# Where the tiles lie in a partition: pools reordered and padded to multiples of 2048 bytes

## The chip, the core and the metric

The kernel runs on one core of a Trainium2 chip. The metric is the device time of one execution in microseconds. Before the change it is 2291.4 us, the median of three runs (2290.7 to 2291.65).

## What is computed

A decoder trunk of two layers on one sequence of 256 positions and 2048 channels, in float32. Each layer normalizes x, projects it with one wide matrix to the queries, keys and values of four kinds of attention (latent, dilated window, forgetting, stick-breaking; four heads of 128 each), joins them through an output projection, and adds a gated FFN of width 5632. Cut to what matters:

```
for l in range(DEPTH):                       # 2 layers
    h = rms_norm(x, attn_norm[l])
    proj = h @ w_in[l]                       # 2048 -> q, k, v of four mixers
    groups = rms_norm(stack(mla, dilated, forgetting, stick_breaking), group_norm[l])
    x = x + groups @ w_out[l]                # 2048 -> 2048
    h = rms_norm(x, ffn_norm[l])
    x = x + (silu(h @ w_gate[l]) * (h @ w_up[l])) @ w_down[l]   # 2048 -> 5632 -> 2048
return rms_norm(x, final_norm)
```

## The kernel before, in words

All 256 positions are held at once, channels on the partitions. The float32 products are made of parts: each operand is split into a high part, rounded to the type float32r, and the low rest, and three of the four partial products are summed in PSUM. So an activation tile holds high and low beside each other (XS for the normalized input of a layer's half, h for everything else that is multiplied: latents, group outputs, FFN activations), and a weight tile comes as a pair wh and wl.

`load` (line 197) fetches the weights in order from one long array: 1 MB at a time into a `raw` tile of 2048 elements for each partition, by SP's queue. ACT then copies it, rounded, to wh (L213), and DVE subtracts to get wl (L214), in two halves of 1024 elements. raw has three buffers, wh and wl four each, so loads run ahead of the matmuls.

All big products go through `Acc.mm` (its matmul is L230), and come in three shapes:

- `wide` (line 241): one weight block of 128x128 is stationary; the moving operand is 512 columns (high and low of an activation) for wh, then 256 columns (the high part) for wl. Used for queries and keys, gate, up and down, and most of the output projection.
- `narrow` (line 234): the same with three matmuls of 256 columns: high and low with wh, high with wl. Used for the latents and for the last quarter of the output and the last chunk of the down projection (`last_out`, line 649, which accumulates in att tiles).
- `proj_v` (line 282): the values. Here the activation is stationary and 512 columns of wh or wl are the moving operand.

FFN: `gate_up` (line 667) makes the h tiles of a chunk of the hidden width from XS (six chunks, of 8 times 128 channels, the last of 4), and the down product of a chunk, with h moving, comes after the next chunk's gate and up.

The pools are opened in lines 170 to 175, and a pool's tiles lie one behind the other in each partition, pools in the order of opening, each tile rounded up to 32 bytes. In the program as built, the first tile X0 starts at byte 16512. That gives these starts before the change:

| tiles | pool | bytes each | first start | past a multiple of 2048 | past a multiple of 64 |
|---|---|---|---|---|---|
| X (8) | cp | 2048 | 16512 | 128 | 0 |
| XS (8) | cp | 4096 | 32896 | 128 | 0 |
| sm, cst, exact | cp | 520, 10264, 1040 | 65664, 66208, 76480 | 128, 672, 704 | 0, 32, 0 |
| raw (3) | rawp | 8192 | 77536 | 1760 | 32 |
| wh, wl (4 each) | wp | 4096 | 102112 | 1760 | 32 |
| h (7) | hp | 4096 | 134880 | 1760 | 32 |
| q4 (4), og | qp | 4096 | 163552 | 1760 | 32 |
| the rest | tp | | 184032 | 1760 | 32 |

All tiles of a pool from rawp to qp have a size that is a multiple of 2048, so all of them lie at the same place as the first.

Of the kernel before, what the change touches and what calls it, by code (L numbers as in the profile page):

```python
# [8 lines left out]
F32 = mybir.dt.float32  # L9
F32R = mybir.dt.float32r  # L10
# [13 lines left out]
LNEXP = "natural_log_exp_and_others"  # L24
SC_A = 192 ** -0.5
SC = 128 ** -0.5
RAW_B, W_B, H_B, Q_B4, OG_B, T2, SG = 3, 4, 7, 4, 1, 3, 3
CH = [8, 8, 8, 8, 8, 4]

# [8 lines left out]
SM_N = SM_FIN + 16  # L38
# [4 lines left out]
C_N = 2566  # L43
# [122 lines left out]
def trunk(ctx: ExitStack, tc: tile.TileContext, x_d, w_d, sm_d, c_d, out_d):  # L166
    nc = tc.nc
    V, A, P = nc.vector, nc.scalar, nc.tensor

    cp = ctx.enter_context(tc.tile_pool(name="cp", bufs=1))  # L170
    rawp = ctx.enter_context(tc.tile_pool(name="rawp", bufs=RAW_B))
    wp = ctx.enter_context(tc.tile_pool(name="wp", bufs=W_B))
    hp = ctx.enter_context(tc.tile_pool(name="hp", bufs=H_B))
    qp = ctx.enter_context(tc.tile_pool(name="qp", bufs=Q_B4))
    tp = ctx.enter_context(tc.tile_pool(name="tp", bufs=2))
    accp = ctx.enter_context(tc.tile_pool(name="accp", bufs=2, space=bass.MemoryType.PSUM))
    attp = ctx.enter_context(tc.tile_pool(name="attp", bufs=4, space=bass.MemoryType.PSUM))

    A.preload_act_table_set(LNEXP)

    X = [cp.tile([128, 2, S], F32, name=f"X{i}") for i in range(8)]
    XS = [cp.tile([128, 2, 2, S], F32R, name=f"XS{i}") for i in range(8)]
    sm = cp.tile([128, SM_N], F32, name="sm")
    cst = cp.tile([128, C_N], F32, name="cst")

    ones = cst[:, C_ONE:C_ONE + 128]
    ident = cst[:, C_ID:C_ID + 128]
    tri = cst[:, C_TRI:C_TRI + 128]

    exact = cp.tile([128, 260], F32R, name="exact")  # L190
    ones_r = exact[:, :128]
    tri_r = exact[:, 132:]

# [67 lines left out]
    def proj_pair(src, nk, per):  # L261
        acc = Acc()
        k = 0
        while k < nk:
            n = min(per, nk - k)
            blk = load(n * 256)
            for kk in range(n):
                for t in range(2):
                    acc.wide(t, blk(kk * 256 + t * 128, 128), src(k), k == nk - 1)
                k += 1  # L270
        return acc

    def proj_quad(src, nk, unit=None, acc=None):
        acc = acc or Acc()
        for k0 in range(0, nk, 4):
            blk = (unit or load)()
            for kk in range(4):
                for t in range(4):
                    acc.narrow(t, blk(kk * 512 + t * 128, 128), src(k0 + kk), k0 + kk == nk - 1)
        return acc.t  # L280
# [17 lines left out]
    def sumsq(srcs):  # L298
        tot = None
        for s in srcs:  # L300
            sq = tp.tile([128, 2, S], F32, name="sq", tag="sg", bufs=SG)
            A.activation(sq, s, AF.Square)
            if tot is None:
                tot = sq
            else:
                V.tensor_add(tot, tot, sq)
        V.tensor_add(tot[:, 0, :], tot[:, 0, :], tot[:, 1, :])
        return tot

    def rsq(tot, n, name, more=None):  # L310
        ps = attp.tile([128, 512], F32, name="att")
        if more is None:
            hl = tp.tile([128, 2, S], F32R, name="ss_hl", tag="hl", bufs=1)
            A.activation(hl[:, 0, :], tot[:, 0, :], AF.Copy)
            V.tensor_sub(hl[:, 1, :], tot[:, 0, :], hl[:, 0, :].bitcast(F32))
            parts, one = [hl[:, 0, :], hl[:, 1, :]], ones_r
        else:
            parts, one = [tot[:, 0, :], *more], ones
        for i, p in enumerate(parts):
            P.matmul(ps[:, :S], one, p, start=i == 0, stop=i == len(parts) - 1)  # L320
        a, ln = tot[:, 1, :], tot[:, 0, :]
        V.tensor_scalar(a, ps[:, :S], 1.0 / n, EPS, op0=OP.mult, op1=OP.add)
        A.activation(ln, a, AF.Ln)
        r0 = tp.tile([128, S], F32, name="rq_r", bufs=1)
        A.activation(r0, ln, AF.Exp, scale=-0.5)
        V.tensor_mul(ln, r0, r0)
        V.scalar_tensor_tensor(a, ln, -0.5, a, op0=OP.mult, op1=OP.mult)
        r = tp.tile([128, S], F32, name=name, bufs=1)
        V.scalar_tensor_tensor(r, a, 1.5, r0, op0=OP.add, op1=OP.mult)
        return r  # L330

    def rcol(r, name):
        ps = attp.tile([128, 512], F32, name="att")
        for t in range(2):
            P.matmul(ps[:, t:t + 1], r[:, t * 128:t * 128 + 128], cst[:, C_SEL + 4:C_SEL + 5],
                     start=t == 0, stop=True, skip_group_check=True)
        c = tp.tile([128, 2], F32, name=name, bufs=1)
        V.tensor_copy(c, ps[:, :2])
        return c

    def split_x(i, g0):
        for t in range(2):
            g = sm[:, g0 + 2 * i + t:g0 + 2 * i + t + 1]
            A.activation(XS[i][:, t, 0, :], X[i][:, t, :], AF.Copy, scale=g)  # L344
            V.scalar_tensor_tensor(XS[i][:, t, 1, :], X[i][:, t, :], g,
                                   XS[i][:, t, 0, :].bitcast(F32),
# [18 lines left out]
    def softmax_heads(qk_mm, vt, scale, mask, o):  # L365
        st = []
        for h in range(4):
            s = tp.tile([128, 384], F32, name="sm_s", bufs=4)
            m = mask(h, s)
            ps = attp.tile([128, 512], F32, name="att")  # L370
            qk_mm(h, ps)
            V.scalar_tensor_tensor(s, ps[:, :384], scale, m, op0=OP.mult, op1=OP.add)
            st.append(s)
        blocks = (slice(0, 128), slice(128, 384))
        for s in st:
            nm = tp.tile([128, 2], F32, name="sm_nm", bufs=4)
            rs = tp.tile([128, 2], F32, name="sm_rs", bufs=4)
            for b, sl in enumerate(blocks):
                V.tensor_reduce(nm[:, b:b + 1], s[:, sl], AX.X, OP.max, negate=True)
            for b, sl in enumerate(blocks):  # L380
                A.activation(s[:, sl], s[:, sl], AF.Exp, bias=nm[:, b:b + 1],
                             accum_out=rs[:, b:b + 1])
            ri = tp.tile([128, 2], F32, name="sm_ri", bufs=4)
            V.reciprocal(ri, rs)
            for b, sl in enumerate(blocks):
                V.tensor_scalar(s[:, sl], s[:, sl], ri[:, b:b + 1], None, op0=OP.mult)
        pst = []
        for s in st:
            pt = attp.tile([128, 512], F32, name="att")
            for j in range(3):  # L390
                P.transpose(pt[:, j * 128:j * 128 + 128], s[:, j * 128:j * 128 + 128], ident)  # L391
            p = tp.tile([128, 384], F32, name="sm_p", bufs=4)
            A.activation(p, pt[:, :384], AF.Copy)
            pst.append(p)
        for h in range(4):
            pv(pst[h], vt, h, o[:, h, :])
# [9 lines left out]
    def qk_plain(qt, kt):  # L406
        def f(h, ps):
            P.matmul(ps[:, :128], qt[:, h, :128], kt[:, h, :128], start=True, stop=True,  # L408
                     skip_group_check=True)
            P.matmul(ps[:, 128:384], qt[:, h, 128:], kt[:, h, :], start=False, stop=True,  # L410
                     skip_group_check=True)
        return f
# [15 lines left out]
    def stick_heads(qt, kt, vt, o):  # L428
        zs, es = [], []
        for h in range(4):  # L430
# [5 lines left out]
            z = tp.tile([128, 384], F32, name="sm_s", bufs=4)  # L436
            V.scalar_tensor_tensor(z, ps[:, :384], SC, cst[:, C_MD:C_MD + 384],
                                   op0=OP.mult, op1=OP.add)
# [21 lines left out]
    def group(og, l, g):  # L460
        tot = sumsq([og[:, 0:2, :], og[:, 2:4, :]])
        r = rsq(tot, GW, "r_g")
        gs = [hp.tile([128, 2, 2, S], F32R, name="h") for _ in range(2)]
        for t in range(4):
            gain = sm[:, l * SM_L + SM_GRP + 4 * g + t:l * SM_L + SM_GRP + 4 * g + t + 1]
            V.scalar_tensor_tensor(og[:, t, :], og[:, t, :], gain, r, op0=OP.mult, op1=OP.mult)
        for t in range(0, 4, 2):
            split(gs[t // 2], og[:, t:t + 2, :])
        return lambda k: gs[k // 2][:, k % 2]

    for l in range(DEPTH):
        sb = l * SM_L
        acc = Acc()
        if l == 0:
            nc.scalar.dma_start(sm, sm_d)

            def first_unit(c=[0]):
# [4 lines left out]
                def x_in(j):  # L482
                    i = i0 + (j - 1 if first else j)
                    if i0 <= i < i0 + 2:
                        nc.sync.dma_start(X[i], x_d[:, 2 * i:2 * i + 2, :])

# [10 lines left out]
        else:  # L497
            proj_quad(xk, KT, None, acc)
        rx = rsq(sumsq(X), D, "r_x")
        rxc = rcol(rx, "rxc")  # L500
# [87 lines left out]
        og = qp.tile([128, 4, S], F32, name="og", bufs=OG_B)  # L588
        softmax_heads(qk_plain(qb, kb), vb, SC, lambda h, s: cst[:, C_MB:C_MB + 384], og)
        grp[1] = group(og, l, 1)  # L590
# [44 lines left out]

        softmax_heads(qk_plain(qc, kc), vc, SC, mask_c, og)
        grp[2] = group(og, l, 2)
# [8 lines left out]
        for p in range(8):  # L646
            proj_pair(lambda k: grp[k // 4](k % 4), 12, 6).add_to(X[p])

# [87 lines left out]
```

## Time and profile before

| | |
|---|---|
| median of three runs | 2291.4 us |
| span of the profiled execution, first to last instruction | 2289.3 us |
| TensorE matmul busy | 2270.7 us (99%) |
| TensorE weight load busy | 2011.0 us (88%) |
| VectorE (DVE) busy | 1538.9 us (67%) |
| ScalarE (ACT) busy | 1107.7 us (48%) |
| bytes moved by DMA | 419.79 MB, mean 183 GB/s |

The profile gives the profiled execution's own time as its span; the median is that of other runs, 2.1 us above it. Matmuls are pipelined: a row's duration overlaps with the next matmul's, and its end is modelled. How fast TensorE really goes is therefore read from the starts of successive matmuls. A tile name such as `acc<-h,wh` names the output, then the moving operand, then the stationary one.

### The profile page before, as it was taken

What the parts mean: (1) busy time and instruction counts of PE and PEld (TensorE: products, weight loads), DVE (VectorE), ACT (ScalarE), POOL (GpSimd) and SP (SyncE); (2) the same over time, 40 slices, a digit from 0 to 9 for tenths busy, and PEclk for the clock granted to TensorE, in tenths of its full rate; (3) what the DMA queues carried; (4) which work ended last, traced back from release to release, by engine and by line L of the source; (5) the groups of instructions that cost most, each with busy time, mean ns of one, the idle gap of its engine ahead of it and who ended that gap; (6) DMA issues with size and microseconds to landing.
All of it is one profiled execution on the core that took longest, in us unless ns stands there. A gap on an engine that the chain in (4) does not pass through costs nothing.

```text
span 2289.3 us, 32935 instructions
## 1 busy us (share of the span) xinstructions
PE 2270.7 (99%) x13462; PEld 2011.0 (88%) x13462; DVE 1538.9 (67%) x1951; ACT 1107.7 (48%) x1425; POOL 0.2 (0%) x4
## 2 busy tenths in 40 slices
PE   8999999999999999999999999999999999999997
PEld 8888889888888888888998988898888888888887
DVE  7876767766656666666777866686656666666666
ACT  6454555544444444444554545565443444444444
POOL 0000000000000000000000000000000000000000
PEclk9999999999999999999999999999999999999999
DMA  7444445555555555555555444455555555555553
GB/s 282 175 166 166 166 149 197 188 192 195 184 185 189 197 184 185 194 189 187 184 185 191 142 173 157 154 203 187 193 193 184 186 190 194 185 186 195 190 184 111
DMA packets 61638, 419.79 MB, mean 183 GB/s; under 512 B 6832, under 2 KB 7088, under 8 KB 14768
## 3 DMA queue, kind: packets, MB, share of 16 engines
q1 hardware_dynamic: 61344, 417.63, 51.2%
q8 instruction: 106, 1.74, 0.3%
q14 instruction: 44, 0.36, 0.0%
q10 hardware_dynamic: 144, 0.07, 0.0%
HBM read 415.57 MB, written 2.10 MB: 182 GB/s over the span
## 4 chain that ended last, share of the span: by engine, by line
PE 99%; DVE 0%; DMA 0%; ACT 0%; DVEq 0%; issue 0%; SPq 0%; ACTq 0%
PE acc L230 92%; PE att L230 4%; PE att L401 1%; PE att L391 0%; PE att L402 0%; PE att L410 0%; PE att L320 0%; DMA X<-in_x_dram 0%; DVE X L701 0%; PE att L408 0%; PE att L422 0%; PE att L432 0%; PE att L424 0%; PE att L629 0%; PE att L420 0%; PE att L434 0%
## 5 line engine op out<-in xcount | busy, mean ns | idle before, releaser
L214 DVE TENSOR_TENSOR wl<-raw,wh 128x1024 fp32r<-128x1024 f32 (+1 forms) x810 | 964.1, 1193 | 657.3 <-ACT wh L213 655.8
L213 ACT ACTIVATE wh<-raw 128x1024 fp32r<-128x1024 f32 (+1 forms) x810 | 838.2, 1036 | 1084.1 <-PE acc L230 953.6
L230 PE MATMUL acc<-XS,wh 128*128 128x512 f32 (+1 forms) x4160 | 1352.0, 377 | 6.3 <-ACT XS L344 6.3
L230 PE MATMUL acc<-XS,wl 128*128 128x256 f32 x3872 | 1086.8, 281 | 0.0
L230 PEld LDWEIGHTS acc<-XS,wh 128*128 128x128 f32 x4160 | 762.6, 188 | 152.8 <-ACT XS L344 6.3
L230 PEld LDWEIGHTS acc<-XS,wl 128*128 128x128 f32 x3872 | 728.5, 188 | 1.0
L230 PE MATMUL acc<-h,wh 128*128 128x512 f32 (+1 forms) x1824 | 619.0, 389 | 0.0
L230 PE MATMUL acc<-h,wl 128*128 128x256 f32 x1744 | 490.9, 281 | 0.0
L230 PEld LDWEIGHTS acc<-h,wh 128*128 128x128 f32 x1824 | 337.9, 188 | 76.3
L230 PEld LDWEIGHTS acc<-h,wl 128*128 128x128 f32 x1744 | 330.0, 189 | 0.3
L230 PE MATMUL acc<-wh,XS 128*128 128x512 f32 x384 | 122.1, 397 | 0.0
L255 DVE TENSOR_TENSOR X<-X,acc 128x512 f32<-128x512 f32 x96 | 66.0, 687 | 44.1 <-PE acc L230 43.8
L230 PE MATMUL att<-h,wh 128*128 128x256 f32 x512 | 92.3, 283 | 0.0
L230 PEld LDWEIGHTS acc<-wh,XS 128*128 128x128 f32 x384 | 72.1, 188 | 17.7
L230 PEld LDWEIGHTS att<-h,wh 128*128 128x128 f32 x512 | 79.9, 192 | 0.2
L251 DVE TENSOR_TENSOR hilo<-acc,lo 128x512 f32<-128x512 f32 x112 | 76.6, 684 | 0.2
L230 PE MATMUL acc<-wl,XS 128*128 128x512 f32 x192 | 75.3, 392 | 0.0
L230 PE MATMUL att<-h,wl 128*128 128x256 f32 x256 | 72.5, 283 | 0.0
L256 DVE TENSOR_TENSOR X<-X,acc 128x512 f32<-128x512 f32 x96 | 65.9, 686 | 2.7
L249 ACT ACTIVATE lo<-acc 128x512 f32<-128x512 f32 x112 | 64.8, 579 | 0.0
L230 PEld LDWEIGHTS att<-h,wl 128*128 128x128 f32 x256 | 49.2, 192 | 0.0
L230 PEld LDWEIGHTS acc<-wl,XS 128*128 128x128 f32 x192 | 36.1, 188 | 8.3
(147 smaller groups left out, 895.9 us busy)
## 6 DMA issues: line engine op xcount, KB each, us to landing
raw<-in_w_dram SPq DMA_DIRECT2D x364, 1024.0 KB, 4.8
raw<-in_w_dram SPq DMA_DIRECT2D x32, 768.0 KB, 4.4
raw<-in_w_dram SPq DMA_DIRECT2D x8, 512.0 KB, 7.8
X<-in_x_dram SPq DMA_DIRECT2D x8, 256.0 KB, 7.1
out_dram<-X SPq DMA_DIRECT2D x8, 256.0 KB, 2.4
cst<-in_const_dram SPq DMA_DIRECT2D x1, 1216.0 KB, 8.9
raw<-in_w_dram SPq DMA_DIRECT2D x4, 256.0 KB, 4.9
cst<-in_const_dram SPq DMA_DIRECT2D x1, 67.0 KB, 7.4
```

What stands on the lines that cost most here:

```text
L213: A.activation(wh[:, i:e], raw[:, o + i:o + e], AF.Copy)
L214: V.tensor_sub(wl[:, i:e], raw[:, o + i:o + e], wh[:, i:e].bitcast(F32))
L230: P.matmul(out, lhsT, rhs, start=bank not in self.started, stop=stop, skip_group_check=True)
L249: A.activation(tmp, self.t[:, :, 1, :], AF.Copy)
L251: V.tensor_add(out, self.t[:, :, 0, :], tmp)
L255: V.tensor_add(x, x, self.t[:, :, 0, :])
L256: V.tensor_add(x, x, self.t[:, :, 1, :])
L401: P.matmul(po[:, :S], vt[0][:, hs], p[:, :S], start=True, stop=False, skip_group_check=True)
```

## The change

Two pools are added. sp, opened first, takes sm and exact, which were in cp, and a tile PAD of 80 float32 that nothing uses; kp, opened between qp and tp, takes cst, which was in cp too. cp keeps X and XS.

```diff
+PAD = 80
+    sp = ctx.enter_context(tc.tile_pool(name="sp", bufs=1))
     cp = ctx.enter_context(tc.tile_pool(name="cp", bufs=1))
     rawp = ctx.enter_context(tc.tile_pool(name="rawp", bufs=RAW_B))
     wp = ctx.enter_context(tc.tile_pool(name="wp", bufs=W_B))
     hp = ctx.enter_context(tc.tile_pool(name="hp", bufs=H_B))
     qp = ctx.enter_context(tc.tile_pool(name="qp", bufs=Q_B4))
+    kp = ctx.enter_context(tc.tile_pool(name="kp", bufs=1))
     tp = ctx.enter_context(tc.tile_pool(name="tp", bufs=2))
...
+    sm = sp.tile([128, SM_N], F32, name="sm")
+    exact = sp.tile([128, 260], F32R, name="exact")
+    sp.tile([128, PAD], F32, name="pad")
     X = [cp.tile([128, 2, S], F32, name=f"X{i}") for i in range(8)]
     XS = [cp.tile([128, 2, 2, S], F32R, name=f"XS{i}") for i in range(8)]
-    sm = cp.tile([128, SM_N], F32, name="sm")
-    cst = cp.tile([128, C_N], F32, name="cst")
+    cst = kp.tile([128, C_N], F32, name="cst")
...
-    exact = cp.tile([128, 260], F32R, name="exact")
```

## Rows read from the trace of the kernel before

**Rows 1.** The page: span, busy us of each engine, share, instructions.

```profile
span 2289.3 us, 32935 instructions
PE 2270.7 (99%) x13462; PEld 2011.0 (88%) x13462; DVE 1538.9 (67%) x1951; ACT 1107.7 (48%) x1425; POOL 0.2 (0%) x4
```

**Rows 2.** The page: the chain that ended last, share by engine, by line.

```profile
PE 99%; DVE 0%; DMA 0%; ACT 0%; DVEq 0%; issue 0%; SPq 0%; ACTq 0%
PE acc L230 92%; PE att L230 4%; PE att L401 1%; PE att L391 0%; PE att L402 0%; PE att L410 0%; PE att L320 0%; DMA X<-in_x_dram 0%; DVE X L701 0%; PE att L408 0%; PE att L422 0%; PE att L432 0%; PE att L424 0%; PE att L629 0%; PE att L420 0%; PE att L434 0%
```

**Rows 3.** Waits of PE: engine and line, what for, total us, times, longest.

```profile
PE acc L230 <- ACT XS L344: 6.3, 1, 6.3
```

**Rows 4.** Groups by form: shapes, count, busy us, mean ns, idle before.

```profile
L230 PE MATMUL acc<-XS,wh 128*128 128x512 f32 x3584 | 1247.5, 392 | 0.0
L230 PE MATMUL acc<-XS,wl 128*128 128x256 f32 x3872 | 1086.8, 281 | 0.0
L214 DVE TENSOR_TENSOR wl<-raw,wh 128x1024 fp32r<-128x1024 f32 x762 | 932.5, 1225 | 650.5 <-ACT wh L213 649.0
...
L230 PEld LDWEIGHTS acc<-XS,wh 128*128 128x128 f32 x4160 | 762.6, 188 | 152.8 <-ACT XS L344 6.3 <-DVE XS L345 0.2
...
L230 PE MATMUL acc<-h,wh 128*128 128x512 f32 x1664 | 589.1, 399 | 0.0
L230 PE MATMUL acc<-h,wl 128*128 128x256 f32 x1744 | 490.9, 281 | 0.0
...
L230 PE MATMUL acc<-wh,XS 128*128 128x512 f32 x384 | 122.1, 397 | 0.0
L230 PE MATMUL acc<-XS,wh 128*128 128x256 f32 x576 | 104.6, 284 | 6.3 <-ACT XS L344 6.3
L230 PE MATMUL att<-h,wh 128*128 128x256 f32 x512 | 92.3, 283 | 0.0
...
L230 PE MATMUL acc<-wl,XS 128*128 128x512 f32 x192 | 75.3, 392 | 0.0
L230 PE MATMUL att<-h,wl 128*128 128x256 f32 x256 | 72.5, 283 | 0.0
L230 PEld LDWEIGHTS acc<-wh,XS 128*128 128x128 f32 x384 | 72.1, 188 | 17.7
...
L230 PE MATMUL acc<-h,wh 128*128 128x256 f32 x160 | 29.9, 286 | 0.0
```

**Rows 5.** PE in order of time, gate and up: start us, us, what.

```profile
701.63 0.39 PE L230 MATMUL acc<-XS,wh 128*128 128x512 f32 x1
...
704.75 0.39 PE L230 MATMUL acc<-XS,wh 128*128 128x512 f32 x1
```

**Rows 6.** PE in order of time, down.

```profile
725.71 0.40 PE L230 MATMUL acc<-h,wh 128*128 128x512 f32 x1
...
728.89 0.40 PE L230 MATMUL acc<-h,wh 128*128 128x512 f32 x1
```

**Rows 7.** The chain in order of time: start us, us, what.

```profile
1119.13 23.04 PE att L230 x192
1142.17 22.53 PE acc L230 x192
```

**Rows 8.** PE in order of time, proj_v of the first mixer (x2: two merged).

```profile
109.66 0.63 PE L230 MATMUL acc<-wh,XS 128*128 128x512 f32 x2
...
112.46 0.63 PE L230 MATMUL acc<-wh,XS 128*128 128x512 f32 x2
```

**Rows 9.** Stretches with XS, h, proj_v: length, then busy by engine, clock, DMA.

```profile
630.00:710.00 80.00, 80.00 (x464) 70.43 (x463) 48.06 (x50) 37.94 (x43) 0.00 (x0) 1.00 0.54 189
718.00:758.00 40.00, 40.00 (x228) 34.73 (x228) 28.20 (x32) 15.48 (x15) 0.00 (x0) 1.00 0.53 185
108.00:127.00 19.00, 19.00 (x83) 15.27 (x82) 11.04 (x13) 7.42 (x7) 0.00 (x0) 1.00 0.56 193
```

**Rows 10.** DMA issues: count, KB each, median us from issue to landing.

```profile
raw<-in_w_dram SPq DMA_DIRECT2D x364, 1024.0 KB, 4.8
```

## The prediction, made before the changed kernel ran

> **What bounds the kernel now.** I read the page's totals first. TensorE is busy for 2270.7 of 2289.3 us, DVE for 67%, ACT for 48%, and the granted clock is 1.00 in the stretches I read [rows 1, 9]. A busy TensorE alone proves little, since the ends of matmuls are modelled, so the chain comes next: it puts 99% of the span on PE and 96% on the one matmul of line 230 [rows 2]. The waits say the same from the other side: PE's one real wait is 6.3 us for the first XS tile at the start [rows 3]. Nothing that feeds PE is ever late. So only two things can move the time: the number of matmuls, which the change leaves alone, and the time from the start of one matmul to the start of the next, which an address might touch.
>
> The durations by form give the first hint that it does [rows 4]. The same 512-column product takes 392 ns when the moving operand is an XS tile and 399 ns when it is an h tile, from the same weight tiles. These durations overlap and their ends are modelled, so I take start-to-start times instead. With XS moving, nine pairs of a 512- and a 256-column matmul take from 701.63 to 704.75: 3.12/9 = 0.3467 us a pair [rows 5]. With h moving, nine pairs take from 725.71 to 728.89: 3.18/9 = 0.3533 [rows 6]. The same split stands in the 256-column products: the chain's stretch of 192 with h takes 23.04 us, 0.1200 each, and that of 192 with XS right behind it 22.53 us, 0.1173 each [rows 7]. The reader is to see a constant toll on h of 6.7 ns a pair and 2.7 ns a narrow matmul, in stretches where PE never waits.
>
> What differs? By the addresses listed ahead, XS starts 128 bytes past a multiple of 2048, while h, wh and wl start 1760 past one, which is 32 bytes past a multiple of 64. Three things could therefore be the cause: the 32 bytes, the fact that h lies at the same place in 2048 as the weights that PE loads beside it, or something that has nothing to do with addresses. A third kind of stretch tells them apart. In proj_v a wh or wl tile is the moving operand and XS the stationary one, so the moving operand has the 32 bytes but lies at another place than its partner. Four rounds of three 512-column matmuls take from 109.66 to 112.46: 2.80/12 = 0.2333 us each [rows 8]. XS at its own rate would need 0.3467 - 0.1173 = 0.2294, h at its own 0.3533 - 0.1200 = 0.2333. proj_v runs at h's rate to the last digit. So I read the toll as one on a moving operand that starts 32 bytes past a multiple of 64. Crossing a 2048 boundary is not it: both halves of an h tile, 1760 (crosses) and 736 (does not), sit in the 0.1200 stretch.
>
> **The change, part by part.** No instruction is added, removed or given a new wait; PAD is never written or read. What moves is addresses. sp holds sm (520 bytes, 544 with rounding), exact (1040, 1056) and pad (320): 1920 in all, so cp starts at 16512 + 1920 = 18432 = 9 x 2048, and X, XS, raw, wh, wl, h, q4 and og all follow at multiples of 2048. cst now stands ahead of tp, which starts 320 bytes later; 320 is a multiple of 64, so tp's tiles keep their 32 bytes and their rates.
>
> 1. Wide products with h moving: 1664 pairs [rows 4] fall from 0.3533 to 0.3467: 1664 x 0.0066 = 11.0 us.
> 2. Narrow products with h moving: 512 + 160 with wh, and for each two of them one with wl (256 + 80): 1008 matmuls, from 0.1200 to 0.1173: 1008 x 0.0027 = 2.7 us.
> 3. proj_v: 384 + 192 matmuls, from 0.2333 to 0.2294: 576 x 0.0039 = 2.2 us. The 48 of the latent values belong here too (0.2 us, within the rounding).
> 4. Products with XS moving go from 128 past 2048 to 0 past it. Both are multiples of 128, so I take 0. Bounds: below nothing by as much as h's toll, 0.0066 on 3584 pairs (23.7 us less) if there were a second step of the same size between 128 and 2048; above nothing by as much, under the first rival.
> 5. The stationary side: wh and wl lose their 32 bytes too. The weight loads take 188 ns whether the tile is wh (32 bytes off) or XS (not off) [rows 4], and proj_v with its aligned weights showed no gain over h without. So I take 0; the bound is again one toll for each pair, (3584 + 1664) x 0.0066 = 34.6 us.
> 6. DVE, ACT and DMA see raw, wh, wl and h at new places. Whatever they gain or lose is hidden by PE: they are at 58 to 71% (DVE), 39 to 47% (ACT) and 0.53 to 0.56 (DMA) in the stretches read [rows 9], and the raw transfer takes 4.8 us against more than 5 us of PE work on one [rows 10]: 16 pairs are 5.55 us. When PE needs 5.55 instead of 5.65 us for such a load, the cover shrinks by 2%. If it went, the next thing late would be DVE's subtraction into wl, whose 1.2 us for a half tile [rows 4] stands against 2.8 us of PE work. Only the 6.28 us before the first matmul are bare to DMA; a transfer 10% faster or slower would move the time by 0.5 us.
> 7. The q4 tiles in attention's float32 products. No aligned row stands beside these, so I take 0 with bounds. All lines but 230 hold 4% of the chain, 92 us [rows 2]; h's toll is 2% of a pair, and on half of these 92 us it would be 1 us either way.
>
> Sum: 11.0 + 2.7 + 2.2 = 15.9 us. The trace's span of 2289.3 becomes 2273.4. The median of the timed runs is 2291.4, 2.1 us above that span; I keep these 2.1 us, since nothing at either end changes: **2275.5 us**, 0.7% less. That one's own range is 2270 to 2280, for which the small terms 6 and 7 and some reading error of the intervals (0.5 ns on the 1664 + 1008 + 576 slow pairs and matmuls, 1.6 us) are taken together.
>
> [...] The trace shows 0.3467 against 0.3533 us for tiles that are all at multiples of 32 bytes [rows 5, 6]. [...]
>
> **The rivals.**
>
> Same place, slower. What slows h could be that it lies at the same place in 2048 as the weights loaded beside it. Then XS, which now has its own place, is brought there too, and would pay h's toll: 3584 x 0.0066 = 23.7 us on the pairs, (576 + 288) x 0.0027 = 2.3 us on its narrow matmuls, with nothing gained elsewhere: 2291.4 + 26 = 2317. It decides from the first gate_up stretch on, where the pair would read 0.3533. For it: h does lie at its weights' place. Against it: proj_v pays the toll although its two operands, 1760 against 128 and steps of 512 from it, never lie nearer than 96 bytes [rows 8]. I give it 8%.
>
> Not the address at all. h's toll could come from what runs beside it: in its stretch DVE is busy for 28.2 of 40 us, with XS for 48.1 of 80 [rows 9]. Then nothing moves: 2291.4. Against it, proj_v has the toll with DVE at 11.0 of 19 us, less than XS has [rows 9]. The case that the allocation comes out otherwise than I reckoned, so that tiles still lie off, ends here too. 11%.
>
> Weights as well. If the stationary side pays a toll of its own that only shows where the moving side is clean, bound 5 comes on top: 2275.5 - 34.6 = 2241. Rows 4 and 8 speak against it. 9%.
>
> Half of it. The toll goes from some of the three kinds alone, say h's pairs keep theirs or only they lose it: 2280 to 2287, 6%.
>
> **How the numbers follow.** The forecast has 66%, and 2275.5 is its time. About 0.2%, 4.6 us, is the least that a measurement of this kernel can tell from no change. Faster by more than that: the forecast, weights as well, and most of the half cases, 0.80. Within it: not the address, 0.11. Slower: same place and what I have not thought of, 0.09. The range for 8 in 10 goes from 2262, which takes in a part of the weights' case, to 2292, which takes in no change; the slower case and the far end of the weights' case stay outside.
>
> **What would show it.** In the changed trace the pairs with h moving should start 0.3467 apart, as those with XS do, the 192 narrow matmuls should take 22.5 us, not 23.04, and proj_v's 0.229 each; XS's pairs should stay at 0.3467, and the weight loads at 188 ns. The forecast is wrong if XS's pairs read 0.3533 (same place), if h's stay there (not the address), if XS's fall (weights), or if the order of matmuls is another one.

## The result: slower, 2309.5 us

The changed kernel takes 2309.54 us (median of five runs, 2308.89 to 2310.01), the kernel before 2291.4: a ratio of 1.008 with a 95% interval of 1.0068 to 1.0093. That is 18.1 us more, where 15.9 less were forecast. The time lies outside the predicted range and on the other side. In both traces every engine executes the same instructions in the same order, PE's long wait is still the 6.3 us at the start, and the granted clock is 0.998; what differs is the addresses.

The page after has the span and the busy time of each engine. Against [rows 1], PE grew by 18.3 us, DVE by nothing.

```profile
span 2307.3 us, 32935 instructions
PE 2289.0 (99%) x13462; PEld 2015.5 (87%) x13462; DVE 1538.9 (67%) x1951; ACT 1106.3 (48%) x1425; POOL 0.2 (0%) x4
```

The groups by form (shapes, count, busy us, mean ns) answer to [rows 4]; L230 is now L234. The 512-column product with XS moving went from 392 to 398 ns, the one with h stayed at 399, and that of proj_v fell from 397 to 389. The weight loads are within 1 ns of where they were.

```profile
L234 PE MATMUL acc<-XS,wh 128*128 128x512 f32 x3584 | 1267.6, 398 | 0.0
...
L234 PEld LDWEIGHTS acc<-XS,wh 128*128 128x128 f32 x4160 | 764.3, 189 | 169.6 <-ACT XS L348 6.3 <-DVE XS L349 0.2
L234 PE MATMUL acc<-h,wh 128*128 128x512 f32 x1664 | 589.3, 399 | 0.0
...
L234 PE MATMUL acc<-wh,XS 128*128 128x512 f32 x384 | 119.3, 389 | 0.0
```

PE in order of time, three stretches of the changed kernel (start us, us, what): gate and up with XS moving, down with h moving, proj_v.

```profile
700.70 0.40 PE L234 MATMUL acc<-XS,wh 128*128 128x512 f32 x1
...
703.88 0.40 PE L234 MATMUL acc<-XS,wh 128*128 128x512 f32 x1
...
730.03 0.40 PE L234 MATMUL acc<-h,wh 128*128 128x512 f32 x1
...
733.21 0.40 PE L234 MATMUL acc<-h,wh 128*128 128x512 f32 x1
```

```profile
109.73 0.62 PE L234 MATMUL acc<-wh,XS 128*128 128x512 f32 x2
...
112.45 0.62 PE L234 MATMUL acc<-wh,XS 128*128 128x512 f32 x2
```

Nine pairs take 3.18 us in both of the first two: 0.3533 a pair, XS now as slow as h, which did not move [rows 5, 6]. Four rounds of proj_v take 2.72 us, 0.2267 a matmul, quicker than the 0.2333 of [rows 8].

The chain of waits of the kernel before, then of the changed one, has the whole FFN but its last product as one unbroken stretch. It shows where the time went.

```profile
422.89 696.25 PE acc L230 x3992
```

```profile
422.80 705.25 PE acc L234 x3992
1128.05 23.04 PE att L234 x192
1151.08 23.04 PE acc L234 x192
```

The stretch holds 1356 pairs with XS and 640 with h. It grew by 9.00 us, and so did its twin in the second layer: 18.0 us, as much as the span. The narrow products with h stayed at 23.04, those with XS rose from 22.53 to 23.04 [rows 7].

One thing does not fit a simple toll. In the same changed kernel, an earlier stretch with XS moving, from the same tiles' places and the same weight buffers' places, runs fast. PE in order of time:

```profile
90.22 0.39 PE L234 MATMUL acc<-XS,wh 128*128 128x512 f32 x1
...
93.34 0.39 PE L234 MATMUL acc<-XS,wh 128*128 128x512 f32 x1
```

Nine pairs in 3.12 us: 0.3467. At the same addresses within 256 bytes, both rates occur.

### The profile page after: what moved, and what is told of

Its sections match the earlier page's. It is cut to its first block, busy times and chain, and to the rows that moved or that the text cites. A ratio compares the mean times of both kernels' runs of the same rounds, so it can differ in the third digit from the quotient of the medians.

```text
span 2307.3 us, 32935 instructions
## 1 busy us (share of the span) xinstructions
PE 2289.0 (99%) x13462; PEld 2015.5 (87%) x13462; DVE 1538.9 (67%) x1951; ACT 1106.3 (48%) x1425; POOL 0.2 (0%) x4
## 4 chain that ended last, share of the span: by engine, by line
PE 99%; DVE 0%; DMA 0%; ACT 0%; DVEq 0%; issue 0%; SPq 0%; ACTq 0%
PE acc L234 92%; PE att L234 4%; PE att L405 1%; PE att L395 0%; PE att L406 0%; PE att L414 0%; PE att L324 0%; DMA X<-in_x_dram 0%; DVE X L705 0%; PE att L412 0%; PE att L426 0%; PE att L436 0%; PE att L428 0%; PE att L633 0%; PE att L424 0%; PE att L438 0%
## 5 line engine op out<-in xcount | busy, mean ns | idle before, releaser
L234 PE MATMUL acc<-XS,wh 128*128 128x512 f32 (+1 forms) x4160 | 1373.6, 383 | 6.3 <-ACT XS L348 6.3
L234 PE MATMUL acc<-XS,wl 128*128 128x256 f32 x3872 | 1090.2, 282 | 0.0
L234 PEld LDWEIGHTS acc<-XS,wh 128*128 128x128 f32 x4160 | 764.3, 189 | 169.6 <-ACT XS L348 6.3
L234 PEld LDWEIGHTS acc<-XS,wl 128*128 128x128 f32 x3872 | 733.0, 189 | 1.1
L234 PE MATMUL acc<-h,wh 128*128 128x512 f32 (+1 forms) x1824 | 619.2, 389 | 0.0
L234 PE MATMUL acc<-h,wl 128*128 128x256 f32 x1744 | 490.7, 281 | 0.0
L234 PEld LDWEIGHTS acc<-h,wh 128*128 128x128 f32 x1824 | 337.9, 188 | 76.7
L234 PEld LDWEIGHTS acc<-h,wl 128*128 128x128 f32 x1744 | 329.7, 189 | 0.3
L234 PE MATMUL acc<-wh,XS 128*128 128x512 f32 x384 | 119.3, 389 | 0.0
L234 PE MATMUL att<-h,wh 128*128 128x256 f32 x512 | 92.3, 283 | 0.0
L234 PEld LDWEIGHTS acc<-wh,XS 128*128 128x128 f32 x384 | 72.1, 188 | 15.2
L234 PEld LDWEIGHTS att<-h,wh 128*128 128x128 f32 x512 | 79.8, 192 | 0.2
L234 PE MATMUL acc<-wl,XS 128*128 128x512 f32 x192 | 74.8, 389 | 0.0
L234 PE MATMUL att<-h,wl 128*128 128x256 f32 x256 | 72.4, 283 | 0.0
L234 PEld LDWEIGHTS att<-h,wl 128*128 128x128 f32 x256 | 49.2, 192 | 0.0
L234 PEld LDWEIGHTS acc<-wl,XS 128*128 128x128 f32 x192 | 36.0, 188 | 7.3
```

The costliest lines, as they stand in the source:

```text
L234: P.matmul(out, lhsT, rhs, start=bank not in self.started, stop=stop, skip_group_check=True)
```

## The experiments

In what follows the distance of a product is the start of its stationary tile minus that of its moving tile, modulo 256. (All blocks of weights, halves of XS and h and so on are steps of multiples of 512, so a product has one distance.) Before, XS had 96, h 0, proj_v 160; in the changed kernel all three have 0. Where a kernel was timed once only, that is marked (one run); the kernel before took 2291.4 (2291.1, 2291.3) us beside them. Repeated runs of one kernel lie within 1.9 us of each other, so larger differences are not chance, and the granted clock was 0.998 in every run.

### All tiles 32 bytes later

```diff
-PAD = 80
+PAD = 88
```

> All tiles from X to og of the changed kernel 32 bytes later, so that XS, wh, wl and h start 32 bytes past a multiple of 2048, all at the same place. Theory P (same place: a moving tile pays 6.7 ns a pair when it starts at the same place, within some block, as the weight tile loaded beside it): nothing changes against the changed kernel, 2309 us, pairs with XS and with h moving 0.3533 us, proj_v 0.227 each. Theory A (own alignment: XS pays because it now starts at a multiple of 2048 itself, or the weights because they start at a multiple of 64): the start is off again, XS pairs return to 0.3467, 2285 to 2291 us.

Measured: 2282.1 us (one run), below both kernels. Both theories missed it. The chain's stretch for the FFN and for the narrow products with XS:

```profile
422.64 691.95 PE acc L234 x3992
...
1137.62 23.04 PE acc L234 x192
```

Narrow products and proj_v (0.227) are exactly as in the changed kernel, as same place said. But the FFN takes 691.95: all 1996 pairs, XS's and h's alike, at 0.3467. So theory P falls in the form in which it was put, and A hardly explains h, which gained as well, or the narrow products, which did not. With the next three runs this led to a third theory, a lock (L in the expectations): at distance 0 two rates hold, and something at the start of a stretch decides which.

### Weights 32 bytes after XS, h 32 after the weights

```diff
+    g0 = ctx.enter_context(tc.tile_pool(name="g0", bufs=1))
+    g0.tile([128, 8], F32, name="gap0")
     rawp = ctx.enter_context(tc.tile_pool(name="rawp", bufs=RAW_B))
...
+    g1 = ctx.enter_context(tc.tile_pool(name="g1", bufs=1))
+    g1.tile([128, 8], F32, name="gap1")
     hp = ctx.enter_context(tc.tile_pool(name="hp", bufs=H_B))
```

> The changed kernel with 32 bytes ahead of raw and 32 more ahead of h: XS at 0, wh and wl at 32, h at 64 past a multiple of 2048. P: XS and h both lie 32 bytes from the weights, both pairs read 0.3467, narrow products 0.1173, proj_v back to 0.2333; 2291.4 - 13.7 = 2278 us. A: XS still starts at a multiple of 2048 and keeps 0.3533; about 2305 to 2310 us.

Measured: 2300.4 us (one run). The chain: FFN, narrow with h, narrow with XS.

```profile
423.57 700.95 PE acc L238 x3992
1124.53 22.40 PE att L238 x192
1146.93 22.72 PE acc L238 x192
```

h at distance 224 is fast (0.3467 a pair, and 22.40/192 = 0.1167 a narrow matmul, better than anything before). XS at 32 is slow, 0.3533, in every stretch of the FFN (one stretch of 21 pairs in a mixer read 0.3469). So being apart is not enough: the two signs of 32 bytes differ. Theory A looked right on XS here, and wrong on h; neither theory had the time.

### Gaps of 64 and 128 bytes

The same edit with 16 and 32 floats in the two gaps.

> 64 bytes ahead of raw and 128 ahead of h: XS at 0, wh and wl at 64, h at 192. P asks how large the block is within which places are compared: if it is 64 bytes, XS and h are both at the same place as the weights and all is as in the changed kernel, 2309 us with pairs at 0.3533; if it is 128, XS is clear (0.3467) and h not (0.3533), 2291 us; if it is 256 or more, both are clear, 2278 us. A: XS keeps 0.3533, 2305 to 2310 us.

Measured: 2303.3 us (one run).

```profile
421.32 703.77 PE acc L238 x3992
1125.09 22.79 PE att L238 x192
1147.87 21.80 PE acc L238 x192
```

XS at distance 64: 0.3533 a pair, yet its narrow products are the quickest of all, 21.80/192 = 0.1135. h at 128: 0.3511 and 0.1187. None of the three cases of theory P came: h's 0.3511 is neither of its rates. But a distance of 128 is not one of 0, so if places are compared within a block, it is larger than 128.

### Gaps of 256 and 512 bytes, XS where it was before

```diff
     cp = ctx.enter_context(tc.tile_pool(name="cp", bufs=1))
+    g0 = ctx.enter_context(tc.tile_pool(name="g0", bufs=1))
+    g0.tile([128, 64], F32, name="gap0")
     rawp = ctx.enter_context(tc.tile_pool(name="rawp", bufs=RAW_B))
...
+    g1 = ctx.enter_context(tc.tile_pool(name="g1", bufs=1))
+    g1.tile([128, 128], F32, name="gap1")
     hp = ctx.enter_context(tc.tile_pool(name="hp", bufs=H_B))
...
-    sp = ctx.enter_context(tc.tile_pool(name="sp", bufs=1))   # was first; now behind qp, without PAD
```

> XS back at 128 as in the kernel before (sm, exact, cst behind og), 256 bytes ahead of raw, 512 ahead of h: wh and wl 256 from XS, h 512 from the weights. P: block of 64, 128 or 256 bytes: both at the same place, 2309 us; block of 512: XS clear, h not, 2291 us; block of 1024 or 2048: both clear, 2278 us. A: XS is where it was before the change, so 0.3467 and 2291 us or less.

Measured: 2309.9 us (one run).

```profile
422.88 705.25 PE acc L237 x3992
...
1151.16 23.04 PE acc L237 x192
```

256 and 512 bytes apart is as good as 0: the FFN stretch has the changed kernel's 705.25 to the last digit, proj_v its 0.227. XS starts at 128 past 2048, as before the change, and is slow all the same, so A falls on XS too. As far as these runs go, the period is 256 bytes.

### sm and exact swapped

Only these two small tiles change place; everything from X to tp stays on the changed kernel's addresses.

```diff
-    sm = sp.tile([128, SM_N], F32, name="sm")
     exact = sp.tile([128, 260], F32R, name="exact")
+    sm = sp.tile([128, SM_N], F32, name="sm")
```

> The changed kernel with sm and exact swapped: exact starts 32 bytes earlier within 256 than in the changed kernel, all tiles from X to tp stay where the change put them, on multiples of 2048. Theory L (lock): the rate hangs on the distance of the stationary from the moving tile, modulo 256; at distance 0 two rates hold, 0.3467 and 0.3533 a pair, and a stretch keeps the one it is in until an odd matmul between (the sums of squares against exact, L324) throws it over. exact's distances are then those of the run with all tiles at 32, so the long FFN stretch should lock at 0.3467 and the time be 2282 us, not 2309. Theory A (own alignment: starting at a multiple of 2048 costs, which is why 32 bytes off was faster): XS, h and weights start as in the changed kernel, so 2309 us.

Measured: 2281.75 us (one run), the 2282 of the lock, and for the FFN stretch

```profile
422.61 691.95 PE acc L234 x3992
```

Nothing that the 1996 pairs read has moved, and they went from 0.3533 to 0.3467. The place where it turns can be seen. At the FFN's start, the two matmuls of a sum of squares against exact (L324) stand among the pairs. PE in order of time, first the changed kernel, then this one:

```profile
418.17 0.40 PE L234 MATMUL acc<-XS,wh 128*128 128x512 f32 x1
...
420.29 0.40 PE L234 MATMUL acc<-XS,wh 128*128 128x512 f32 x1
...
420.89 0.28 PE L324 MATMUL att<-ss_hl,exact 128*128 128x256 f32 x1
...
421.47 0.40 PE L234 MATMUL acc<-XS,wh 128*128 128x512 f32 x1
...
422.17 0.39 PE L234 MATMUL acc<-XS,wh 128*128 128x512 f32 x1
...
422.52 0.28 PE L324 MATMUL att<-ss_hl,exact 128*128 128x256 f32 x1
...
423.33 0.40 PE L234 MATMUL acc<-XS,wh 128*128 128x512 f32 x1
...
426.16 0.40 PE L234 MATMUL acc<-XS,wh 128*128 128x512 f32 x1
```

```profile
417.98 0.40 PE L234 MATMUL acc<-XS,wh 128*128 128x512 f32 x1
...
420.10 0.40 PE L234 MATMUL acc<-XS,wh 128*128 128x512 f32 x1
...
420.69 0.28 PE L324 MATMUL att<-ss_hl,exact 128*128 128x256 f32 x1
...
421.27 0.40 PE L234 MATMUL acc<-XS,wh 128*128 128x512 f32 x1
...
421.98 0.40 PE L234 MATMUL acc<-XS,wh 128*128 128x512 f32 x1
...
422.34 0.28 PE L324 MATMUL att<-ss_hl,exact 128*128 128x256 f32 x1
...
422.80 0.40 PE L234 MATMUL acc<-XS,wh 128*128 128x512 f32 x1
...
426.27 0.39 PE L234 MATMUL acc<-XS,wh 128*128 128x512 f32 x1
```

Both arrive slow: six pairs in 2.12 us, 0.3533. In the changed kernel the first L324 throws the stream into the fast rate (two pairs in 0.70) and the second throws it back (eight pairs in 2.83, 0.354), and there it stays for the 700 us of the FFN. With exact 32 bytes earlier the first leaves it slow (two pairs in 0.71) and the second throws it into the fast rate (ten pairs in 3.47, 0.347), and there it stays. Two pairs are few to read a rate from, but the two rates have different patterns: slow pairs take 361, 349 and 350 ns in turn, fast ones, in these stretches, 345 to 348 each. Between the two L324 three pairs take 348, 351 and 347 ns in the changed kernel, and 341, 351 and 361 here; the second layer repeats both to within 1 ns.

sm moved as well, but it is hardly the cause. In the run with all tiles 32 bytes later, sm and exact stayed and the rest moved by 32 bytes: there exact lies to the rest, modulo 256, as it does here, sm does not, and the FFN stretch is the same 691.95.

### The kernel before with 32 bytes ahead of h

```diff
+    g0 = ctx.enter_context(tc.tile_pool(name="g0", bufs=1))
+    g0.tile([128, 8], F32, name="gap0")
     hp = ctx.enter_context(tc.tile_pool(name="hp", bufs=H_B))
```

> The kernel before with a gap of 32 bytes ahead of h: XS stays 96 bytes (modulo 256) from its weights, h goes from 0 to 224, the distance at which the run with w at 32 and h at 64 had 0.3467 a pair and 0.1167 a narrow matmul. L: 1664 pairs gain 0.0066 each, 1008 narrow matmuls 0.0033: 2291.4 - 11.0 - 3.3 = 2277 us, faster than both kernels. A: h now starts at 1792, a multiple of 256, and would keep its toll or gain nothing: 2289 to 2292 us.

Measured: 2278.22 us against 2291.05 beside it, ratio 0.9945 (0.9928 to 0.9961); 2277 was expected. h at distance 224 is fast, wherever it starts itself: the FFN stretch reads

```profile
420.40 692.01 PE acc L232 x3992
```

### The distances 160 and 192

The edit of the gaps ahead of raw and h again: 40 and 16 floats, then 48 and 24.

> The changed kernel with gaps, so that the weights are 160 bytes (modulo 256) after XS and 192 after h. L: one steady rate for each distance, no change of rate within a stretch; which one is open, between 0.3467 and 0.3533 for each: 2275 to 2312 us, proj_v (distance 96) between 0.227 and 0.2333. A: XS at a multiple of 2048 keeps 0.3533, over 2300 us.

> The two distances swapped: weights 192 bytes after XS and 160 after h. L: the rates that the run with 160 and 192 shows for XS and h change places, to within 0.2 ns a pair: what h had at 192, XS has now, and the other way round; proj_v (distance 64) between 0.227 and 0.2333. A: XS at a multiple of 2048 keeps 0.3533, over 2300 us.

Measured: 2303.3 and 2308.7 us (one run each). The chain of the first, then of the second:

```profile
424.84 700.74 PE acc L238 x3992
1125.58 22.61 PE att L238 x192
1148.19 23.04 PE acc L238 x192
```

```profile
425.10 703.12 PE acc L238 x3992
1128.22 23.04 PE att L238 x192
1151.25 22.62 PE acc L238 x192
```

The rates change places as the lock theory said. Over whole FFN stretches of 127 to 459 pairs, distance 160 gives 0.3500 a pair for XS in the first run and 0.3500 to 0.3501 for h in the second; 192 gives 0.3533 for h and 0.3532 to 0.3533 for XS; the narrow products' 22.61 and 23.04 swap as well. In the FFN the rate belongs to the distance, not to the tile or its data. Two things were not as expected: proj_v at distance 96 took 0.2342 in the first run, a little over the upper bound of 0.2333, and in the second run XS at 192 read 0.3489 to 0.3492 in three stretches outside the FFN (22 to 82 pairs), so a distance other than 0 can have a second rate too.

### Three more for a layout and a control

All distances 224 (56 floats ahead of raw, 8 ahead of h); exact first with 8 floats ahead of h; and 24 floats ahead of raw, which has the distances of the kernel before with XS on multiples of 2048.

> The changed kernel with 224 bytes ahead of raw and 32 ahead of h: the weights lie 224 bytes (modulo 256) after XS and after h. L: pairs 0.3467 for both, narrow matmuls 0.1167 for both; against the run with 32 bytes ahead of h (2278 us) XS's 864 narrow matmuls gain 1.5 us, and proj_v at distance 32, not seen yet, lies between 0.227 and 0.2343, 3.9 us better to 0.6 worse: 2273 to 2278 us. A: XS on a multiple of 2048 pays, 2300 us or more.

> The run with exact first (2281.8 us), and 32 bytes ahead of h: XS at distance 0, where both rates hold and proj_v is quickest, h at 224, which knows the fast rate alone. L: h pulls the FFN into the fast rate, and XS keeps it when its turn comes; 336 narrow rounds with h gain 0.0098 each, 3.3 us, some 200 pairs with h outside the FFN 1 us: 2277 to 2278 us, all FFN pairs at 0.3467. If the lock isn't kept over a change of tile, XS's FFN pairs go back to 0.3533 after h, 2290 to 2300 us.

> Control: the changed kernel with 96 bytes ahead of raw: XS on multiples of 2048, but the distances are those of the kernel before, weights 96 after XS and 0 from h. L: XS pairs 0.3467, h pairs 0.3533 in the FFN, proj_v 0.2333, so the time of the kernel before, 2291 us within 2. A (XS pays on a multiple of 2048): 2305 us or more.

Measured: 2276.91 us, ratio to before 0.9935 (0.9921 to 0.995), within what was expected; 2277.64 us, ratio 0.994 (0.9923 to 0.9956), also as expected; and 2290.2 us (one run) for the control, the time of the kernel before within 1.2 us. The FFN stretch of each in the same order:

```profile
421.03 691.95 PE acc L238 x3992
...
1135.38 22.40 PE acc L238 x192
```

```profile
421.65 692.01 PE acc L236 x3992
```

```profile
422.74 696.24 PE acc L236 x3992
```

In the first the pairs of XS and h both run fast, and no stretch showed a second rate. In the second XS at distance 0 keeps the fast rate each time that it takes over from h in the FFN. That is not so in general: in the kernel before, h at distance 0 takes over from XS at 0.3467 and runs at 0.3533 [rows 5, 6], without an odd matmul between. What decides there was not found. The control repeats the 696.25 of before although XS now lies on multiples of 2048: XS's own alignment, at which the change aimed, costs nothing, the distances do. The first layout is the best version seen and beats both kernels, by 14 and 33 us. Its proj_v, at distance 32, runs at 0.2333 like that of before; the second has proj_v at 0.227 but XS's narrow products at 23.03. I did not look for a layout with both.

## Why the prediction was wrong

**What bounds the kernel** was right. PE's pace is the time: DVE, ACT and DMA saw their tiles move and nothing came of it, as step 6 said: DVE is busy for 1538.9 us in both traces, ACT for 1107.7 and 1106.3, and a raw transfer lands in 4.8 and 4.7 us. Nor did the q4 tiles of step 7 count: attention's 256-column products with q last 379 to 381 ns on average before and 379 to 380 after. The weights' own alignment (step 5) costs nothing, as was said: with all distances at 0, weights at 32 past 2048 (all tiles later) and at 0 (exact first) both gave 691.95 us for the FFN stretch.

**Steps 1 and 2** (h gains 11.0 and 2.7 us) failed: nothing was gained, the pairs took 0.3 us more. h and its weights kept their distance of 0, and with it 0.3533 and 23.04. The start of h is not what it pays for: at multiples of 2048 it stayed slow in the changed kernel, and at 32 past one, with distance 224, it was fast in the run with exact first and 8 floats ahead of h.

**Step 3** (proj_v gains 2.2): the sign was right, but by luck. From 0.2333 to 0.2271 over a whole proj_v stretch, 576 matmuls gained 3.6 us; the 48 of the latent values, which read h at distance 0 before and after, gained less than 0.1. But the cause is the distance, 160 to 0: with all tiles 32 bytes later, and so the moving tile 32 past a multiple of 64 again, proj_v kept 0.2271.

**Step 4** (XS moves from 128 to 0 and nothing happens) is the step whose failure turned the sign: a term put at nothing measured 21.6 us. What counted was not XS's start but its distance from the weights, 96 to 0. That brought it from a distance with one fast rate to one with two, and the FFN fell into the slow one: 2 x 9.00 us. From start to start over the whole of both traces, XS's 3584 pairs take 20.0 us more, with the 18.0 in them; narrow products with XS add 1.6, h's pairs 0.3, and proj_v gives 3.6 back. That is 18.3 us; the span grew by 18.0, since 0.3 less passed after the last matmul.

**The false inference**, on which steps 1 to 4 rest, stood ahead of them: the toll was read as one on a moving tile that starts 32 bytes past a multiple of 64. proj_v was to tell the 32 bytes from the same place, because its operands lie apart and it runs at h's rate "to the last digit". It does, at 0.2333, but as another distance with a rate of its own, 160; the agreement was chance. Three stretches, with the distances 96, 0 and 160, could not carry a law of addresses: h and proj_v shared the moving tile's start and, by chance, the rate, and XS differed from both in its start and in its distance at once.

**The rivals.** Same place, at 8%, named the tile, the stage and the price: XS's FFN pairs at 0.3533, h unchanged. It said 2317, since it had no proj_v gain and let all pairs of XS pay, where those of several mixer stretches stayed fast. It is not the law either: with everything at the same place, the runs with all tiles 32 bytes later and with exact first were some 27 us faster than the changed kernel. "Not the address at all" is out: moving tiles in steps of 32 bytes gave times from 2276.91 to 2309.9 us.

**What stays open** is why. The rate of these matmuls hangs on where the stationary tile lies against the moving one (346.7 to 353.3 ns a pair), with a period of 256 bytes as far as the run with gaps of 256 and 512 shows (705.25 us for the FFN stretch, as at 0), and at distance 0 a stretch can hold one of two rates, 346.7 or 353.3. No run here shows how PE reads the two tiles, nor what in the odd matmul throws the stream over.

## What to carry to other kernels

Where PE is the bound and never waits, read the start-to-start time of the same product with different tiles: a constant difference may be an address at work (0.3467 against 0.3533 us here). Between the best and the worst layout here it is worth 33 us. Choose the distance of stationary and moving tiles, by a few bytes of padding between pools, rather than the alignment of either; and prefer a distance at which only one rate was seen (224 here), since at one with two an unrelated small tile can cost or give 1%, as the swap of sm and exact did (2309.54 to 2281.75 us). Any edit that moves a tile may shift such rates, so compare them before a gain or loss is put down to what the edit meant to do.

## What the runs showed that was not expected

The rates by distance, in ns, over all runs of this case. A pair is 512 + 256 columns, a narrow round 3 x 256, a proj_v round 3 x 512. Pairs are means of starts over FFN stretches of 127 pairs or more, narrow rounds and proj_v those over whole stretches of 192 and 96 matmuls.

| distance | pair | narrow round | proj_v round | seen with |
|---|---|---|---|---|
| 0 | 346.7 or 353.3 | 360 | 681 | h before; all in the changed kernel |
| 32 | 353.3 | 355 | 700 | XS, weights 32 after it |
| 64 | 353.3 | 341, some 353 | 700 | XS, weights 64 after it |
| 96 | 346.7 | 352 to 356, some 360 | 703 | XS before |
| 128 | 351.1 | 356 | not seen | h, 128 after the weights |
| 160 | 350.0 | 360 | 700 | XS and h; proj_v before |
| 192 | 353.3 | 353 | 687 | h and XS |
| 224 | 346.7 | 350 | 700 | h and XS |

proj_v holds XS still and moves the weights, so its distance is XS's with the sign turned round, and its column comes from other runs than the tiles named beside it.

The same mean hides different rhythms. In the FFN 353.3 ns are pairs of 361, 349 and 350 in turn at distance 0, of 345 to 346 and 360 to 361 in turn at 32, and of 353 to 354 each at 64. The fast 346.7 is 346 to 347 on almost every pair for XS at 96 and at 224.

The spread is 2% for pairs and 6% for narrow rounds, and no distance is best for all three shapes. Smaller steps than 32 bytes were not tried.
